# Expert weights in 2 MB tiles, and 21 buffers of 8 KB regrouped as ten of 16 KB and one of 8 KB

## The chip, the cores and the metric

One NeuronCore of a Trainium2 chip runs the kernel: TensorE (PE; its weight loads are listed as PEld), VectorE (DVE), ScalarE (ACT), GpSimd (POOL), SyncE (SP, which issues most transfers here), and 16 DMA engines that move data between HBM and the core's memory of 128 partitions. The metric is the device time of one execution in microseconds, lower being better. The kernel before was timed three times: 1330.16, 1330.19 and 1331.1 us, median 1330.19 us.

## What is computed

One decoder layer for 256 tokens of width 1024, all weights in float32: a combined projection, a Mamba-2 mixer and a sliding-window attention side by side, a gated merge, an output projection, and a mixture of 32 experts of which each token takes 4. Cut to what matters here:

```python
p = x @ W_in                      # 1024 -> [z | xBC | dt | q | k | v | gate_ssm | gate_attn]
s = mamba2(z, xBC, dt)            # causal conv, chunked scan, gate, RMS norm
a = sliding_window_attention(q, k, v)
m = (sigmoid(gate_ssm) * (s @ P_ssm) + sigmoid(gate_attn) * (a @ P_attn)) @ W_o
h = layer_norm(alpha * x + m)
# experts: top 4 of 32
hgu = h[tokens of e] @ w_gate_up[e] + b_gate_up[e]      # 1024 x 2048 per expert: 8 MB
act = glu * sigmoid(1.702 * glu) * (lin + 1)
y_e = act @ w_down[e] + b_down[e]                       # 1024 x 1024 per expert: 4 MB
y   = layer_norm(alpha * h + sum_k gate_k * y_e(k))
```

The expert weights are 32 x 12 MB, 402.65 million bytes; everything else that is loaded is about 60 million bytes.

## The kernel before, in words

**Buffers.** Nearly everything large lies in one pool of 21 buffers of 8 KB per partition (1 MB each, `gtile`): raw weight tiles as they land, their split parts, activations, and later the expert weights. A buffer is handed on when the last instruction on it has run, and the transfer or the write that takes it next waits for that.

**The first stages.** The list `stream` holds 50 weight tiles of 1 MB for the projections: 34 of `w_in` (k, v, then c and q mixed, eight of z, eight of g), 4 of `w_attn_out`, 8 of `w_ssm_out` (tiles 38 to 45) and 4 of `w_mix` (tiles 46 to 49). For float32 accuracy each raw tile is split in two: ACT writes `whi` (rounded), DVE writes `wlo` = raw - `whi`, and PE multiplies three products (`mm3`). `take()` hands PE the next tile: in `weights`, SP is first told to load up to `ahead` tiles further, and `split_ahead` then emits the splits up to `la` tiles further (2 in most stages, 1 in the z stage, 4 at the end). Small pieces of the mixer and the attention are emitted between the matmuls of the weight tiles (`tick`, `side`), always in the order of the program on each engine.

**The end of the first stages.** In the loop over `n` PE takes the eight `w_ssm_out` tiles; `merge` then puts the two branches together on DVE and ACT. After that SP loads x, the norm's constants, the router's weights and `b_down`, and PE runs `mix(c, q)`, for two halves `c` of the tokens and four weight tiles `q`, all four of which stay in memory until `mix(1, q)` has used them. Then come the norm, the router (`turn`, `logits`, `top`, `place`) and the first `gather`, in which PE picks the tokens of two experts by a one-hot matrix.

**The experts.** Tiles of 1 MB: 8 per expert for gate and up (`u`, 128 rows of 2048 each, so 8 KB in one run per partition), 4 for down (`d`, 256 rows, two neighbouring rows per partition, 8 KB in one run). The order is u of expert 0, u of expert 1, d of expert 0, u of expert 2, d of expert 1, and so on. SP loads 6 and then 14 of them during the mix stage (`MB`, `PRE`), and keeps 17 ahead from then on (`AH`, 6 near the end, `AL`). The last tile is loaded in two halves. After the last d tile PE adds the last expert's share, and DVE normalises and stores (lines 1185 to 1200).

Of the kernel before, what the change touches and what calls it, by code (L numbers as in the profile page):

```python
# [8 lines left out]
F = mybir.dt.float32  # L9
# [6 lines left out]
P = 128  # L16
D = 1024
# [10 lines left out]
NGRAN = 21  # L28
AH = 17
MA, MB = 4, 6  # L30
# [3 lines left out]
OVER, AL = 27, 6  # L34
DT, DD = 2, 4
D3 = 4
PRE = 14
L1 = 2
AZ, LZ, AG, LG = 2, 1, 3, 2
# [6 lines left out]
def hybrid_layer(ctx, tc, x, w_in, conv_w, conv_b, dt_bias, a_log, d_skip, norm_w, w_ssm_out,  # L46
# [5 lines left out]
    gran = ctx.enter_context(tc.tile_pool(name="gran", bufs=NGRAN))  # L52
# [40 lines left out]
    st = {"dma": 0, "split": 0, "ahead": 3, "la": 1}  # L93
    raws, splits = {}, {}

    def prefetch(upto):
        while st["dma"] < min(upto, len(stream)):
            i = st["dma"]
            ap, nb = stream[i]
            t = gtile(f"raw{i}")  # L100
            t3 = t.rearrange("p (k n) -> p k n", n=nb)
            if len(halves(i)) > 1:
                nk = 2048 // nb // 2
                for k in (slice(0, nk), slice(nk, 2 * nk)):
# [20 lines left out]
    def weights(i):  # L125

        prefetch(i + 1 + st["ahead"])
        if i >= S_E:
            return raws.pop(i).rearrange("p (k n) -> p k n", n=1024)
        split_ahead(i)  # L130
        nb = stream[i][1]
        return tuple(t.rearrange("p (k n) -> p k n", n=nb) for t in splits.pop(i))

    def split_ahead(i):
# [42 lines left out]
    for e in range(NE + 1):  # L177
        for kp in range(8 if e < NE else 0):
            slots.append(("u", e, kp))
            add(w_gate_up[0, e, P * kp:P * (kp + 1)].rearrange("p (h n) -> p h n", h=2), 1024)  # L180
        for kp in range(4 if e else 0):
            slots.append(("d", e - 1, kp))
            add(w_down[0, e - 1, 256 * kp:256 * (kp + 1)].rearrange("(p j) n -> p j n", j=2), 1024)
# [20 lines left out]
    xn = gtile("xn")  # L204
    xn3 = xn.rearrange("p (c d) -> p c d", d=D)
    for c in range(2):
        nc.sync.dma_start(xn3[:, c], x[0, c * P:(c + 1) * P])
    prefetch(2)
# [38 lines left out]
    ii = const.tile([P, 64], F, name="ii")  # L247
    tt(ii, ident[:, 0:64], ident[:, 64:128], OP.add)


    xh = gtile("xh", R).rearrange("p (k t) -> p k t", t=NT)
    xl = gtile("xl", R).rearrange("p (k t) -> p k t", t=NT)
# [144 lines left out]
    BC = gtile("BC").rearrange("p (s g t) -> p s g t", s=2, g=4)  # L397
    xs = [gtile(f"xs{c}") for c in range(2)]
    xd = [gtile(f"xd{c}") for c in range(2)]
# [43 lines left out]
    cb_t = gtile("cbm").rearrange("p (s g t) -> p s g t", s=4, g=4)  # L443
# [27 lines left out]

    def build_a(c, g):
        ah = gtile(f"ah{c}{g}", R)
# [5 lines left out]
        return ah4  # L479

    def ssd(c, g):
        gcs = slice(512 * g, 512 * g + 512)
        yield need(0, ah=1, xe=1 - c)
        ah4 = build_a(c, g)
# [12 lines left out]
        later(1, lambda: done(bank=2, ah=1))  # L497
# [32 lines left out]
    qT = gtile("qT").rearrange("p (b t) -> p b t", t=NT)  # L530
    kv_t = gtile("kv")
# [4 lines left out]
    def attention(kv, b):  # L536
# [83 lines left out]
    sz = []  # L620
# [3 lines left out]
    def gated():  # L624
# [6 lines left out]
        nwb = gtile("nwb")  # L631
        nc.sync.dma_start(nwb, rows(norm_w, DI))
        yield need(1)
        nc.scalar.preload_act_table_set(EXP_LN)
# [3 lines left out]
        for g in range(4):  # L638
            gcs = slice(512 * g, 512 * g + 512)
            if g % 2 == 0:  # L640
                yT[g // 2] = [gtile(f"yt{g}{p_}", R).rearrange("p (b t) -> p b t", t=NT) for p_ in "hl"]
# [17 lines left out]
    st["la"], st["ahead"], st["rate"] = L1, 3, R1  # L659
# [7 lines left out]
    for kind, j in ORDER:  # L667
# [17 lines left out]
        elif kind == "g":  # L685
            if j == 0:
                st["ahead"], st["la"] = AG, LG
            if j % 4 == 0:
                gts.append(gtile(f"gate{j}").rearrange("p (b t) -> p b t", t=NT))
# [17 lines left out]
        else:  # L707
            if j == 0:
                st["rate"], st["ahead"], st["la"] = R2, AZ, LZ
                sz.extend(gtile(f"sz{c}") for c in range(2))  # L710
                start(0, gated())
# [20 lines left out]
    bgn = gran.tile([32, 2048], F, name="bgn", tag="g")  # L732
    nc.sync.dma_start(bgn, b_gate_up[0])
    mrg = gtile("mrg").rearrange("p (b t) -> p b t", t=NT)
# [18 lines left out]
    mh = gtile("mh", R).rearrange("p (b t) -> p b t", t=NT)  # L753
    ml = gtile("ml", R).rearrange("p (b t) -> p b t", t=NT)
# [7 lines left out]

    for n in range(4):
# [467 lines left out]
```

## Time and profile before

| | us |
|---|---|
| median of three runs | 1330.19 |
| the profiled execution | 1330.74 |
| its span in the profile | 1329.0 |
| PE busy in the span | 1251.8 |
| DVE busy | 431.6 |
| ACT busy | 281.2 |
| first matmul with expert weights | 388.35 |
| DMA: moved in the span | 463.34 MB |

The profile is one execution; its span starts with the first instruction and is 1.2 us shorter than the median of the runs. PE's busy time overlaps itself, since matmuls are pipelined, so a PE that is shown busy is not a PE that could do no more. The DMA rows give what the 16 engines moved in each fortieth of a stretch. A row of the timeline is: start, length, engine, line, operation, what it writes and reads, how many such instructions were put together, and in brackets how long the engine sat idle before it and what ended that.

### The profile page before, as it was taken

To read this page: it belongs to the slowest core of one execution; us is meant where nothing else is said; L and a number is where in the kernel's file an instruction comes from. 1 tells how busy PE (TensorE), PEld (TensorE's weight loads), DVE (VectorE), ACT (ScalarE), POOL (GpSimd) and SP (SyncE) were. 2 spreads that over 40 slices of the span, in tenths; PEclk is the share of its full clock that TensorE was granted. 3 is DMA by queue.
4 is the path that set the end of the run, shared out by engine and by line. 5 is a ranking of instruction groups with operands and counts; after the bars stand their busy time and mean duration, and the time that the engine had idled before them with its cause. 6 is when DMAs were issued, how large, how long until landed. Compare 5 with 4: busy or idle time off the path is not lost. (4 is left out here: it accounts for less than half of the span.)

```text
span 1329.0 us, 16490 instructions
## 1 busy us (share of the span) xinstructions
PE 1251.8 (94%) x6864; PEld 668.7 (50%) x6864; DVE 431.6 (32%) x817; ACT 281.2 (21%) x477; POOL 63.1 (5%) x35
## 2 busy tenths in 40 slices
PE   7999999999999999999999989899898989879985
PEld 7998878999864344343343323333242323223321
DVE  6998987665631211111112111111111111111114
ACT  5555555543211110011010101001010101000001
POOL 0044332000000000000000000000000000000000
PEclk9999999999989999999999999999999999989998
DMA  9523334655999999999999999999999999999994
GB/s 302 181 64 105 118 122 147 208 183 186 354 420 418 422 421 420 421 421 420 421 421 421 421 421 420 421 421 421 421 421 421 421 421 421 420 417 421 420 421 197
DMA packets 106232, 463.34 MB, mean 349 GB/s; under 512 B 9948, under 2 KB 48996, under 8 KB 56964
## 3 DMA queue, kind: packets, MB, share of 16 engines
q1 hardware_dynamic: 106148, 462.19, 86.8%
q8 instruction: 57, 0.93, 0.3%
q14 instruction: 27, 0.22, 0.0%
HBM read 461.11 MB, written 1.05 MB: 348 GB/s over the span
## 5 line engine op out<-in xcount | busy, mean ns | idle before, releaser
L76 PE MATMUL u<-raw,xg 128*64 128x512 f32 x2048 | 470.4, 600 | 29.9 <-DMA raw<-in_w_gate_up_dram 29.8
L76 PEld LDWEIGHTS u<-raw,xg 128*64 128x64 f32 x2048 | 137.7, 137 | 331.3 <-issue 233.8
L76 PE MATMUL d<-raw,ac 128*64 128x512 f32 x1024 | 245.9, 606 | 18.7 <-DMA raw<-in_w_down_dram 10.4
L992 DVE COPY gu<-u 128x512 f32<-128x512 f32 x32 | 22.1, 691 | 701.3 <-PE u L76 701.3
L76 PEld LDWEIGHTS d<-raw,ac 128*64 128x64 f32 x1024 | 67.2, 137 | 147.8 <-issue 104.8
L65 DVE TENSOR_TENSOR wlo<-raw,whi 128x2048 fp32r<-128x2048 f32 (+1 forms) x51 | 120.4, 2371 | 13.2 <-ACT whi L62 12.9
L76 PE MATMUL ws<-xh,whi 128*128 128x256 f32 x400 | 101.7, 292 | 1.8 <-ACT whi L62 1.8
L62 ACT ACTIVATE whi<-raw 128x2048 fp32r<-128x2048 f32 (+1 forms) x51 | 95.4, 1875 | 28.5 <-DMA raw<-in_w_in_dram 8.0
L76 PE MATMUL ws<-xl,whi 128*128 128x256 f32 x400 | 98.3, 283 | 0.0
L62 ACT ACTIVATE gu<-u 128x512 f32<-128x512 f32 x32 | 19.1, 597 | 333.5 <-PE u L76 333.5
L76 PEld LDWEIGHTS ws<-xh,whi 128*128 128x128 f32 x400 | 76.9, 192 | 4.3 <-ACT whi L62 2.2
L76 PEld LDWEIGHTS ws<-xl,whi 128*128 128x128 f32 x400 | 76.9, 192 | 0.9 <-issue 0.7
L76 PEld LDWEIGHTS xg<-G,xr 128*128 128x128 f32 x512 | 61.8, 197 | 24.9 <-issue 24.3
L76 PE MATMUL xg<-G,xr 128*128 128x128 f32 x512 | 67.9, 287 | 0.2 <-DVE G L65 0.2
L62 ACT ACTIVATE xg<-xg 128x512 f32<-128x512 f32 x32 | 19.1, 597 | 215.0 <-PE xg L76 215.0
L76 PE MATMUL out<-y,S 64*128 64x512 f32 x256 | 63.6, 615 | 0.8 <-ACT y L62 0.8
L76 PE MATMUL ws<-xh,wlo 128*128 128x256 f32 x400 | 56.2, 283 | 0.0
L62 ACT ACTIVATE hg<-hg 128x512 f32<-128x512 f32 x32 | 20.2, 631 | 149.8 <-DVE hg L69 149.8
L76 PEld LDWEIGHTS ws<-xh,wlo 128*128 128x128 f32 x400 | 51.6, 192 | 0.0
L1004 PEld LDWEIGHTS tu<-ident,gu 128*128 128x128 f32 x256 | 33.2, 208 | 26.3 <-issue 25.2
L1085 POOL IOTA omisc<- 128x192 f32 x1 | 0.3, 295 | 928.4 <-PE u L76 928.4
L76 PEld LDWEIGHTS out<-y,S 64*128 64x128 f32 x256 | 22.0, 186 | 41.9 <-issue 40.2
(248 smaller groups left out, 1172.1 us busy)
## 6 DMA issues: line engine op xcount, KB each, us to landing
raw<-in_w_gate_up_dram SPq DMA_DIRECT2D x256, 1024.0 KB, 19.8
raw<-in_w_down_dram SPq DMA_DIRECT2D x127, 1024.0 KB, 19.8
raw<-in_w_in_dram SPq DMA_DIRECT2D x33, 1024.0 KB, 5.3
raw<-in_w_ssm_out_dram SPq DMA_DIRECT2D x8, 1024.0 KB, 5.1
raw<-in_w_attn_out_dram SPq DMA_DIRECT2D x4, 1024.0 KB, 5.1
raw<-in_w_mix_out_dram SPq DMA_DIRECT2D x4, 1024.0 KB, 5.1
xn<-in_x_dram SPq DMA_DIRECT2D x2, 512.0 KB, 3.8
raw<-in_w_in_dram SPq DMA_DIRECT2D x2, 512.0 KB, 6.1
```

What stands on the lines that cost most here:

```text
L62: return nc.scalar.activation(o, i, func, **kw)
L65: return nc.vector.tensor_tensor(o, a, b, op=op)
L76: return nc.tensor.matmul(o, l, r, start=start, stop=stop)
L992: nc.vector.tensor_copy(t, banks[hf])
L1004: nc.tensor.transpose(pb[:, b], gu[hf][:, o:o + 255:2], ident)
L1085: nc.gpsimd.iota(ios, pattern=[[ns, 2], [1, ns]], base=cap, channel_multiplier=0, allow_small_or_imprecise_dtypes=True)
```

## The change

The pool becomes ten buffers of 16 KB per partition (`ptile`), mostly used as `pair`: two tiles of 8 KB that are taken and given back together (hi and lo of a weight tile, x's two parts, the two gates, and so on), and one lone buffer of 8 KB (`single`: x at first, then k and v, then the residual). Raw weight tiles of the first stages no longer take pool buffers: they alternate between the two halves of one pair, `ring`, and tile i + 2 is loaded when tile i has been split. `la` is 1 from the first tile to the last. An expert tile is 2 MB: two neighbouring gate-and-up rows or four neighbouring down rows per partition, 16 KB in one run, fetched by one transfer; the columns that PE picks from `hn` and `gu` step by 2 and by 4 accordingly. Loads of expert tiles are asked for at places written out by hand (`prefetch(1)` to `prefetch(10)`). The loads of x, the norm's constants and the router's weights (`mix_loads`) move ahead to the third round of the loop over n; `norm_w` is loaded by ACT's queue into the place of `sz[0]`, `b_down` by GpSimd's. The last expert tile is loaded as 1 MB and two halves of 0.5 MB.

```diff
-NGRAN = 21
-AH = 17
-MA, MB = 4, 6
+NPAIR = 10
+AH = 9
-OVER, AL = 27, 6
+OVER, AL = 27, 7
-PRE = 14
-L1 = 2
-AZ, LZ, AG, LG = 2, 1, 3, 2
+L1 = 1
+LZ, LG, LS = 1, 1, 1
...
-    def gtile(name, dt=F):
-        return gran.tile([P, 2048], dt, name=name, tag="g")
+    def ptile(name, dt=F):
+        return gran.tile([P, 4096], dt, name=name, tag="g")
+
+    def pair(name, dt=F):
+        t = ptile(name, dt)
+        return t[:, 0:2048], t[:, 2048:4096]
...
+    single = lone.tile([P, 2048], F, name="single")
+    ring = pair("ring")
+
+    def prefetch_raw():
+
+        while st["dma"] < S_E:
             i = st["dma"]
             ap, nb = stream[i]
+            if i - 2 >= st["split"]:
+                break
+            t = ring[i % 2]
...
+    def prefetch(upto):
+
+        while moe[0] < min(upto, len(stream) - S_E):
+            m = moe[0]
+            ap, nb = stream[S_E + m]
+            t = ptile(f"w{m}").rearrange("p (k n) -> p k n", n=nb)
+            last = S_E + m == len(stream) - 1
+            for ks in (slice(0, 2), slice(2, 3), slice(3, 4)) if last else (slice(0, 4096 // nb),):
+                nc.sync.dma_start(t[:, ks], ap[:, ks])
+            raws[S_E + m] = t
+            moe[0] += 1
...
-        prefetch(i + 1 + st["ahead"])
-        if i >= S_E:
-            return raws.pop(i).rearrange("p (k n) -> p k n", n=1024)
+        prefetch_raw()
         split_ahead(i)
+        prefetch_raw()
...
+    def expert_weights(n):
+
+        m = n // 2
+        prefetch(m + 1 + st["ahead"])
...
-            hi, lo = gtile(f"whi{j}", R), gtile(f"wlo{j}", R)
+            hi, lo = pair(f"w{j}", R)
...
-            add(w_gate_up[0, e, P * kp:P * (kp + 1)].rearrange("p (h n) -> p h n", h=2), 1024)
+            add(w_gate_up[0, e, 256 * kp:256 * (kp + 1)].rearrange("(p j) n -> p j n", j=2), 2048)
...
-            add(w_down[0, e - 1, 256 * kp:256 * (kp + 1)].rearrange("(p j) n -> p j n", j=2), 1024)
+            add(w_down[0, e - 1, 512 * kp:512 * (kp + 1)].rearrange("(p j) n -> p j n", j=4), 1024)
...
+    st["la"] = LS
     for n in range(4):
+        prefetch((0, 1, 2, 2)[n])
...
+        if n == 2:
+            xr, lnc, wr3, br = mix_loads()
...
             if n == 3 and kh == 1:
-                st["la"] = 4
+                prefetch(3)
...
+        if q == 0:
+            prefetch(4)
     mix(1, 0)
     first_norm(0)
+    prefetch(5)
     mix(1, 1)
     resid(1, 0)
-    prefetch(S_E + MB)
+    prefetch(6)
     mix(1, 2)
+    prefetch(7)
     mix(1, 3)
     resid(1, 1)
+    prefetch(10)
...
-                kk = slice((4 * kq + k) * P, (4 * kq + k + 1) * P)
+                o = 256 * (2 * kq + k // 2) + k % 2
                 for c in range(2):
-                    mm(pb[:, k], hn[:, c, kk], G2[:, c], c == 0, c == 1)
+                    mm(pb[:, k], hn[:, c, o:o + 255:2], G2[:, c], c == 0, c == 1)
```

## Rows read from the trace of the kernel before

**Rows 1.** The page's span and the rate of transfers in 40 equal slices.
```profile
span 1329.0 us, 16490 instructions
...
GB/s 302 181 64 105 118 122 147 208 183 186 354 420 418 422 421 420 421 421 420 421 421 421 421 421 420 421 421 421 421 421 421 421 421 421 420 417 421 420 421 197
```

**Rows 2.** Busy time of each engine by stretch; last PE's clock, DMA share, GB/s.
```profile
33.00:166.00 133.00, 128.89 (x1008) 119.97 (x1007) 124.49 (x211) 74.29 (x151) 43.57 (x21) 0.97 0.38 118
166.00:266.00 100.00, 99.94 (x652) 86.91 (x651) 71.77 (x80) 56.74 (x92) 18.63 (x8) 1.00 0.50 159
266.00:347.00 81.00, 81.00 (x677) 80.83 (x676) 48.26 (x56) 33.46 (x33) 0.00 (x0) 1.00 0.61 202
...
410.00:1300.00 890.00, 842.10 (x4006) 313.51 (x4004) 133.56 (x350) 87.28 (x154) 0.29 (x1) 0.99 1.01 421
```

**Rows 3.** Timeline of SP's queue: the issues of two successive experts' gate-and-up tiles.
```profile
562.74 17.72 SPq L107 DMA_DIRECT2D raw<-in_w_gate_up_dram  x8
...
592.56 5.30 SPq L107 DMA_DIRECT2D raw<-in_w_gate_up_dram  x3
```

**Rows 4.** Timeline of PE at the first expert matmuls.
```profile
388.35 3.65 PE L76 MATMUL u<-raw,xg 128*64 128x512 f32 x16
391.93 1.98 PE L76 MATMUL out<-xr,ia 128*128 128x512 f32 x4
```

**Rows 5.** Transfers from 342 to 410 us: the ordinary queue's packets, MB, share.
```profile
q1 hardware_dynamic: 5422, 27.83, 101.1%
```

**Rows 6.** Timeline of PE at the last expert's tiles.
```profile
1303.56 1.94 PE L76 MATMUL d<-raw,ac 128*64 128x512 f32 x8 [0.65 <-DMA raw<-in_w_down_dram]
...
1309.58 3.65 PE L76 MATMUL d<-raw,ac 128*64 128x512 f32 x16
...
1313.99 1.99 PE L76 MATMUL out<-y,S 64*128 64x512 f32 x8 [0.76 <-ACT y L62]
```

**Rows 7.** Packets moved from 560 to 900 us, by size.
```profile
DMA packets 19641, 143.14 MB, mean 421 GB/s; under 512 B 2181, under 2 KB 2181, under 8 KB 2181
```

**Rows 8.** Transfers from 14 to 34 us, tiles of w_in alone: rate in 40 slices, packets.
```profile
GB/s 92 281 371 389 389 373 352 350 348 352 346 348 344 371 338 348 352 356 350 346 348 350 346 348 346 350 346 350 350 346 346 354 346 348 346 346 350 348 352 344
DMA packets 6800, 6.88 MB, mean 344 GB/s; under 512 B 96, under 2 KB 6799, under 8 KB 6799
```

**Rows 9.** The page's transfers by name: count, KB each, median us from issue to landing.
```profile
raw<-in_w_ssm_out_dram SPq DMA_DIRECT2D x8, 1024.0 KB, 5.1
...
xr<-in_x_dram SPq DMA_DIRECT2D x1, 1024.0 KB, 4.9
```

**Rows 10.** Timeline of DVE: the wlo of tile 5, and of tiles 44 and 45.
```profile
37.63 2.28 DVE L65 TENSOR_TENSOR wlo<-raw,whi 128x2048 fp32r<-128x2048 f32 x1
...
326.23 4.49 DVE L65 TENSOR_TENSOR wlo<-raw,whi 128x2048 fp32r<-128x2048 f32 x2
```

**Rows 11.** Timeline of PE: first matmuls that read the wlo of tiles 5 and 45.
```profile
45.71 1.12 PE L76 MATMUL ws<-xh,wlo 128*128 128x256 f32 x8
...
343.53 1.12 PE L76 MATMUL yss<-yt2h,wlo 128*128 128x256 f32 x8
```

**Rows 12.** Timeline of all engines around the mix stage.
```profile
347.37 0.40 PE L76 MATMUL mix<-whi,mh 128*128 128x512 f32 x1
...
349.49 1.92 ACT L62 ACTIVATE whi<-raw 128x2048 fp32r<-128x2048 f32 x1 [1.67 <-DMA raw<-in_w_mix_out_dram]
...
352.08 4.48 DVE L65 TENSOR_TENSOR wlo<-raw,whi 128x2048 fp32r<-128x2048 f32 x2
...
354.42 0.50 PE L76 MATMUL mix<-wlo,mh 128*128 128x512 f32 x1 [1.20 <-DVE wlo L65]
```

**Rows 13.** Timeline of PE: the transposes that follow the last matmul of the mix stage.
```profile
370.65 1.03 PE L851 MATMUL ht<-ident,xr 128*128 128x128 f32 x8
```

**Rows 14.** The page's weight loads of PE with adjoining columns (xg) and with every second (tu).
```profile
L76 PEld LDWEIGHTS xg<-G,xr 128*128 128x128 f32 x512 | 61.8, 197 | 24.9 <-issue 24.3
...
L1004 PEld LDWEIGHTS tu<-ident,gu 128*128 128x128 f32 x256 | 33.2, 208 | 26.3 <-issue 25.2
```

More of the change, by code (lines that the diff above doesn't have):

```diff
@@ L246, in hybrid_layer @@
         nc.vector.memset(io64[:, :, cap:], -5.0)
[L247 to L252, printed above, removed]
+    xh, xl = (t.rearrange("p (k t) -> p k t", t=NT) for t in pair("x", R))
     xb = [bank(f"xt{kk}").rearrange("p (k c t) -> p k c t", k=2, c=2) for kk in range(4)]
@@ L394, in dt_chain @@
         sub_lo(avl, av, avh)
-    BC = gtile("BC").rearrange("p (s g t) -> p s g t", s=2, g=4)
-    xs = [gtile(f"xs{c}") for c in range(2)]
-    xd = [gtile(f"xd{c}") for c in range(2)]
+    sz = pair("sz")
+    BC = sz[1].rearrange("p (s g t) -> p s g t", s=2, g=4)
+    qT, cb_t = pair("qcb")
+    qT = qT.rearrange("p (b t) -> p b t", t=NT)
+    xs = pair("xs")
+    xd = pair("xd")
     def conv_block(blk, ps, dst):
@@ L470, in decays @@
         act(dte, pa[:, 32:64], AF.Exp)
+    ahs = []
     def build_a(c, g):
-        ah = gtile(f"ah{c}{g}", R)
+        if "ah" not in ready:
+            ready.add("ah")
+            ahs.extend(pair("ah", R))
+        ah = ahs.pop(0)
         ah4 = ah.rearrange("p (s h t) -> p s h t", s=2, h=8)
@@ L630, in gated @@
                 later(1, lambda v=v, w=w, k=k: act(w, v, AF.Square, accum_out=ss[:, k:k + 1]))
-        nwb = gtile("nwb")
-        nc.sync.dma_start(nwb, rows(norm_w, DI))
         yield need(1)
+        nwb = sz[0]
+        nc.scalar.dma_start(nwb, rows(norm_w, DI))
         nc.scalar.preload_act_table_set(EXP_LN)
@@ L640, in gated @@
             if g % 2 == 0:
-                yT[g // 2] = [gtile(f"yt{g}{p_}", R).rearrange("p (b t) -> p b t", t=NT) for p_ in "hl"]
+                yT[g // 2] = [t.rearrange("p (b t) -> p b t", t=NT) for t in pair(f"yt{g}", R)]
             for c in range(2):
@@ L656, in gated @@
                 later(1, ev)
-    st["la"], st["ahead"], st["rate"] = L1, 3, R1
+    st["la"], st["rate"] = L1, R1
     gts = []
@@ L686, in hybrid_layer @@
             if j == 0:
-                st["ahead"], st["la"] = AG, LG
-            if j % 4 == 0:
-                gts.append(gtile(f"gate{j}").rearrange("p (b t) -> p b t", t=NT))
+                st["la"] = LG
+                gts.extend(t.rearrange("p (b t) -> p b t", t=NT) for t in pair("gate"))
             def ev(b, ps, j=j):
@@ L708, in hybrid_layer @@
             if j == 0:
-                st["rate"], st["ahead"], st["la"] = R2, AZ, LZ
-                sz.extend(gtile(f"sz{c}") for c in range(2))
+                st["rate"], st["la"] = R2, LZ
                 start(0, gated())
@@ L729, in hybrid_layer @@
             later(2, lambda j=j: ready.add(("z", j)))
-    bgn = gran.tile([32, 2048], F, name="bgn", tag="g")
+    bgn, mrg = pair("mrg")
+    bgn = bgn[0:32]
     nc.sync.dma_start(bgn, b_gate_up[0])
-    mrg = gtile("mrg").rearrange("p (b t) -> p b t", t=NT)
+    mrg = mrg.rearrange("p (b t) -> p b t", t=NT)
     for n in range(4):
@@ L820, in hybrid_layer @@
     posm = const.tile([P, 2, 32], F, name="posm")
-    ones = rt[:, 416:544]
     ia = const.tile([P, P], F, name="ia")
-    lg, mk, rp, ex = (rt[:, 544 + 64 * i:608 + 64 * i].rearrange("p (c e) -> p c e", c=2) for i in range(4))
-    t8, nm, sw = rt[:, 800:816].rearrange("p (c e) -> p c e", c=2), rt[:, 816:818], rt[:, 818:820]
+    ones = const.tile([P, P], F, name="ones")
+    lg, mk = (const.tile([P, 2, 32], F, name=n) for n in ("lg", "mk"))
+    nm, sw = (const.tile([P, 2], F, name=n) for n in ("nm", "sw"))
+    rp, ex = s64("rp").rearrange("p (c e) -> p c e", c=2), gw
+    t8 = s64("t8")[:, 0:16].rearrange("p (c e) -> p c e", c=2)
     ts(ia, ident, ALPHA, None, OP.mult)
@@ L1181, in hybrid_layer @@
             done_d(n, e, cur[0], S)
-    lnd = gtile("lnd").rearrange("p (s d) -> p s d", d=D)
-    nc.sync.dma_start(lnd[:, 0], rows(ln2_g, D))
-    nc.sync.dma_start(lnd[:, 1], rows(ln2_b, D))
-    res = gtile("res").rearrange("p (c d) -> p c d", d=D)
+    lnd, res = (t.rearrange("p (s d) -> p s d", d=D) for t in pair("lnd"))
+    lnd = [lnd[:, 0], lnd[:, 1]]
+    nc.sync.dma_start(lnd[0], rows(ln2_g, D))
+    nc.sync.dma_start(lnd[1], rows(ln2_b, D))
     work = mo
```

153 lines of the change are left out of this document (74 added, 79 removed).

## Prediction

> **What bounds the kernel now.** I read the transfers first. From the tenth slice on they run at about 420 GB/s without a break [rows 1], and from 410 to 1300 us the DMA engines are fully busy while PE, busy time included that only overlaps, is not [rows 2]: the expert stage is bound by the loading of 402.65 MB. One expert's 12.58 MB come every 29.82 us [rows 3], which is 422 GB/s, or 2.485 us for a tile of 1 MB. Before 347 us the picture is the other way round: the transfers run at 118 to 202 GB/s and PE has hardly a gap [rows 2]; that part is bound by PE, with DVE close behind it from 33 to 166 us (124.5 of 133 us, 94%). So the time is the time at which PE gets through the first stages, then the time to load what is not yet in memory, then a tail. A gain must come from loading faster or from having more loaded when the expert stage begins; and what makes PE late in the first stages is paid in full, unless memory holds more by then.
>
> **How much is loaded at the start.** PE begins with the experts at 388.35 us and has used up 2 MB of them at 391.93 [rows 4]. From 342 to 410 us the ordinary queue moved 27.83 MB [rows 5]; 1.05 MB of it is the last mix tile and some 0.4 MB the remainder of the loads before it, so about 26.4 MB of expert weights are in at 410. The other 376.3 MB end with the last half tile. The first d tile of the last expert is waited for until shortly before 1303.56 [rows 6]; three tiles more at 2.485 us make that last landing 1310.9. So 376.3 MB take 900.9 us, starts, stutters and the uneven finish of the engines included.
>
> After the change all ten pairs go to experts: 20.97 MB fit, no more. They are full before PE is done with its first 2 MB tile (see the mix stage below), so that the eleventh tile can only be asked for when 16 matmuls are through, where the old kernel was loading all along. Had it been full at the same moment, about 18.8 MB would have been in (26.4 less 18.1 us at 422 GB/s), so that the preload is worth some 2 MB, or 5 us, not the three tiles that are fetched early. PE releases the next tiles every 4.5 to 5.5 us (16 matmuls are 3.58 us, and the residual adds 1.9 [rows 4]), about what a transfer of 2 MB takes, so little is lost after that.
>
> **Larger packets.** Each transfer ran in packets of 8 KB, and each adds one tiny packet per DMA engine: from 560 to 900 us 17,460 large ones and 2,181 small [rows 7], 8 and 1 per engine and MB. Tiles of 16 KB per partition would halve both: 9 packets fewer per engine and 2 MB. What is a packet's fixed price? Tiles of w_in come in packets of 1 KB, and where these fill the engines the rate settles at 348 GB/s [rows 8]: 3.01 us per MB with 64 packets per engine, against 2.485 us with 8. The difference, 0.53 us over 56 packets, is 9.4 ns each: 85 ns per 2 MB tile, 1.7%, and 15.5 us over the 182 tiles that follow the first ten. From below: a lone MB in 1 KB packets lands in 5.1 us, one in 4 KB packets in 4.9 [rows 9]; that is 4 ns each, or 7 us in all; and nothing at all if long runs are cut at 8 KB. A loss is excluded: fewer packets of the same engines have no price of their own in any row. I take 9.4 ns, since that stretch has full engines as the expert stage has.
>
> [...]
>
> **What the first stages lose.** (a) *Lookahead 1 and two pairs for split weights.* For each of the tiles 2 to 45 I read in the timelines how long before PE's first use its wlo was finished. With lookahead 2 that was 5 to 16 us: 5.8 for tile 5, done at 39.9 and used at 45.7, and 12.8 for tile 45, done at 330.7 and used at 343.5 [rows 10, 11]. One tile less takes a tile's period from this (5.8 to 13 us). What is left is 0 to 7 us for c and q tiles, and 1.4 to 7 us for g to `w_ssm_out`. The z tiles already had lookahead 1 and PE lost nothing there [rows 2]. In the c and q stage DVE has 8.5 us of slack in all [rows 2]; if waiting for whi leaves it idle, PE waits. Bounds 0 and 8.5 us; I take 3.
>
> (b) *The end of the first stages.* In the mix stage PE needs a tile every 2.73 us (12 matmuls), while a tile needs ACT for 1.9 and DVE for 2.24 us, and the load of mix tile 3 now waits until tile 1 in the same half of the ring is split. The chain from 347.4, when PE starts mix tile 0 and frees a pair: whi of tile 1 until 349.3, the last `merge` about 1 us, wlo until 352.5, load of tile 3 5.1 us, whi and wlo until 361.8; then PE has that tile and the second half's four left, 13.6 us: 375.4. The old kernel split these tiles ahead, lost 1.2 us [rows 12] and ended at 370.65 [rows 13]. That is 4.8 us. Before it, SP now puts 4.3 MB (an expert tile, x, the norm's constants, the router: some 10 us of transfers) ahead of the raw tile 45, which can be asked for at about 329, when tile 43 is split, and which PE wants split from 341.6 on: 0 to 4 us more. SP issues in order, so an expert tile without a free pair holds up the raw tile behind it; the third one waits for the pair that PE frees with tile 44 at 341.6, and holds mix tile 3, which waits longer for the ring anyway. I take 6.5 for the whole, bounds 3 and 9. The expert tiles that are asked for on the way (at about 311, 323, 346, 353 and 362, then as pairs are freed up to 375) are all in by about 398.
>
> (c) *Strided columns.* The 32 matmuls of the first gather read every second column; such a weight load takes 208 ns, an even one 197 [rows 14]: 0.4 us. Later ones lie under the transfers.
>
> (d) *No price, with their cover:* `norm_w` is asked for on ACT's queue one step (2.9 us of PE) before DVE reads it, and a lone MB lands in 5.1 us [rows 9]: at worst 2.2 us of DVE, which has 28 of 100 us idle there [rows 2]. `b_down` is asked for on an idle GpSimd before the experts begin.
>
> **The tail.** With 2 MB the last but one tile holds two quarters of the last expert, and lands whole 4.9 us before the last piece. Then come four times 1.94 us of d, 1.99 of out and 0.44 of S: 10.2 us, so PE ends 5.3 us after the last landing, where it was 2.3 (1309.58 + 3.65 [rows 6], against 1310.9). The remaining 15.8 us to the span's end stay. Price 3 us.
>
> **The sum.** First release 391.93 + 0.4 + 3 + 6.5 = 401.8. Issue and first byte 1.8 (most of the 2.1 by which a lone MB's 5.1 us exceed its 3.0): 403.6. The remaining 381.7 MB at the old pace 913.8, less 15.5 for packets: 898.3, so the last landing is at 1301.9. Tail 5.3 + 15.8: the span is 1323.0. The profiled execution took 1330.74 for its 1329.0 of span; the median lies 1.2 above the span: **1324 us**, 6 us or 0.5% less.
>
> **The rivals.**
> - *Packets save next to nothing* (runs cut at 8 KB, or a price that grows with bytes): then the sum gives 1324 + 15.5 = 1339, slower. It decides from a saving below 51 ns per tile, at which 1330 is reached. For it: lone transfers show 4 ns (1332). Against it: the full engines' 348 against 422 GB/s. This is also how the change would fail to do what it says.
> - *DVE becomes the bound of the c and q stage*, because each split now waits for a pair and for PE: 8.5 us instead of 3, and 9 instead of 6.5 in (b): 1332. For it: 94% busy [rows 2]. Against it: the z stage.
> - *The first stages lose next to nothing*, splits being hidden as in the z stage and only the mix chain costing 3 us: 1324 - 6.5 = 1317. For it: PE's waits on splits are short now. Against it: the mix chain above.
>
> **How the numbers follow.** My forecast has 48% (1318 to 1329), the first rival 17% (1331 to 1339), the second 17% (1329 to 1335), the third 18% (1312 to 1318). The range 1313 to 1337 leaves out the outer ends of the first and third rival. A measurement here can tell about 0.2% from no change, so faster is under 1327.5: most of the forecast (41%) and the third rival, 59%. Within 0.2%: the rest of the forecast and parts of the first two rivals, 18%. Slower, above 1332.9: 23%.
>
> **What would show it.** Packets of 16 KB and about 4.92 us between issues of expert tiles, 428 GB/s where it was 421; a dip of the transfers just before the first expert tile is released, at about 402 us; PE idle before wlo in the mix stage and `ht` at 377 to 380 us; some idle DVE before 166 us; the last d matmul some 5 us behind the last landing. I am wrong if the rate stays at 422 GB/s, if `ht` starts before 373 or after 385, or if PE rather than the transfers ends the expert stage.

## The result, and the profile after

| kernel | us, median (lowest to highest) | against before (95% interval) |
|---|---|---|
| before | 1330.59 (1330.16 to 1331.10) | |
| changed | 1339.11 (1337.41 to 1339.88) | 1.0062 (1.0045 to 1.0080) |
| predicted | 1324 (1313 to 1337) | |

The change makes the kernel 8.5 us slower, where 6 us less were forecast; the time lies outside the range. The profiled execution took 1339.34 us for a span of 1337.6. First the page of the changed kernel, to set beside [rows 1]: span, rate of transfers in 40 equal slices, packets.

```profile
span 1337.6 us, 16127 instructions
...
GB/s 227 159 126 97 121 99 126 189 166 238 319 342 335 383 429 431 431 431 430 430 430 430 430 430 431 430 430 431 430 431 431 431 431 430 431 427 430 430 430 172
DMA packets 78741, 463.30 MB, mean 346 GB/s; under 512 B 6908, under 2 KB 45956, under 8 KB 53924
```

From the fifteenth slice on the loads are faster than before, 430 against 421. The loss lies between slices 11 and 14, at 319 to 383, where the old kernel ran at 354 and then 420. The same by stretches, to set beside [rows 2] (stretch, length, busy time of PE, its weight loads, DVE, ACT and POOL, then PE's granted clock, DMA share, GB/s):

```profile
33.00:166.00 133.00, 126.63 (x992) 118.12 (x990) 123.57 (x208) 75.67 (x151) 43.04 (x19) 0.97 0.40 124
166.00:266.00 100.00, 98.29 (x606) 83.94 (x607) 65.51 (x79) 51.59 (x89) 21.29 (x10) 0.97 0.45 144
266.00:347.00 81.00, 81.00 (x676) 80.52 (x675) 49.42 (x55) 33.56 (x35) 0.00 (x0) 1.00 0.66 227
347.00:410.00 63.00, 48.45 (x245) 40.15 (x244) 30.69 (x62) 13.68 (x16) 1.16 (x2) 0.86 0.86 332
410.00:460.00 50.00, 50.00 (x235) 21.08 (x236) 9.28 (x30) 7.30 (x13) 0.00 (x0) 0.97 0.89 335
460.00:1300.00 840.00, 800.26 (x3836) 305.56 (x3834) 121.23 (x318) 81.41 (x145) 0.30 (x1) 1.00 1.01 430
```

The kernel before, from 347 on:

```profile
347.00:410.00 63.00, 59.21 (x273) 38.40 (x273) 23.30 (x63) 10.00 (x18) 0.00 (x0) 0.93 1.01 419
410.00:460.00 50.00, 50.00 (x248) 20.09 (x246) 11.63 (x30) 5.55 (x10) 0.00 (x0) 0.99 1.01 419
```

PE idles 14.6 of the 63 us from 347 on, where it had idled 3.8, and the DMA engines stand too (0.86, then 0.89, where they had been at 1.01). Its timeline there (start, length; in brackets the idle time before and what ended it), to set beside [rows 4, 12, 13]:

```profile
353.68 2.57 PE L79 MATMUL yss<-yt,w 128*128 128x256 f32 x16 [3.65 <-ACT w L65]
...
366.74 5.58 PE L79 MATMUL mix<-w,m 128*128 128x512 f32 x23 [2.16 <-DVE w L68]
376.72 0.79 PE L79 MATMUL mix<-w,m 128*128 128x512 f32 x1 [4.40 <-ACT w L65]
379.05 15.31 PE L79 MATMUL mix<-w,m 128*128 128x512 f32 x59 [1.53 <-DVE w L68]
...
394.20 1.03 PE L883 MATMUL ht<-ident,single 128*128 128x128 f32 x8
...
411.90 3.65 PE L79 MATMUL u<-w,xg 128*64 128x512 f32 x16
415.49 1.98 PE L79 MATMUL out<-single,ia 128*128 128x512 f32 x4
```

Each wait up to 379 us is for a split weight tile. `ht` starts 23.5 us later than in [rows 13], the first expert matmul 23.5 us later than in [rows 4]. The expert period on SP's queue, to set beside [rows 3]: 29.12 us, where it was 29.82.

```profile
773.28 14.87 SPq L126 DMA_DIRECT2D w<-in_w_gate_up_dram  x4
...
802.40 0.33 SPq L126 DMA_DIRECT2D w<-in_w_gate_up_dram  x1
```

And the tail, to set beside [rows 6]:

```profile
1312.02 1.94 PE L79 MATMUL d<-w,ac 128*64 128x512 f32 x8 [0.81 <-DMA w<-in_w_down_dram]
...
1318.04 3.65 PE L79 MATMUL d<-w,ac 128*64 128x512 f32 x16
1322.45 1.99 PE L79 MATMUL out<-y,S 64*128 64x512 f32 x8 [0.76 <-ACT y L65]
```

**Where the 8.5 us come from.** From 415 to 460 us the ordinary queue moved 15.52 MB on top of the ten tiles (20.97 MB), so 36.5 MB are in at 460. Before, it moved 20.91 MB from 410 to 460, on top of some 26.4: 47.3 MB. The 10.8 MB that are missing are 25 us of loading. The other 366 MB (29.1 experts) come 0.70 us per expert sooner: 20.4 us. The tail is 3 us longer. 25 - 20.4 + 3 is some 8 us, of 8.5 measured. So the change gave what was hoped for from loading, and gave back more ahead of it. Two questions follow: what makes the first stages late, and what makes the loads faster.

### The profile page after: what moved, and what is told of

The parts are those of the page before. It is cut to its first block, busy times and chain, and to the rows that moved or that the text cites. A ratio compares the mean times of both kernels' runs of the same rounds, so it can differ in the third digit from the quotient of the medians.

```text
span 1337.6 us, 16127 instructions
## 1 busy us (share of the span) xinstructions
PE 1252.5 (94%) x6864; PEld 682.1 (51%) x6864; DVE 431.6 (32%) x816; ACT 282.9 (21%) x477; POOL 66.4 (5%) x37
## 5 line engine op out<-in xcount | busy, mean ns | idle before, releaser
L79 PE MATMUL u<-w,xg 128*64 128x512 f32 x2048 | 464.5, 598 | 22.1 <-DMA w<-in_w_gate_up_dram 22.1
L79 PEld LDWEIGHTS u<-w,xg 128*64 128x64 f32 x2048 | 140.2, 137 | 314.7 <-issue 263.5
L79 PE MATMUL d<-w,ac 128*64 128x512 f32 x1024 | 241.1, 602 | 19.7 <-DVE gg L73 10.3
L79 PE MATMUL ws<-x,w 128*128 128x256 f32 x1200 | 154.9, 289 | 2.8 <-ACT w L65 2.5
L79 PEld LDWEIGHTS ws<-x,w 128*128 128x128 f32 x1200 | 149.3, 195 | 6.1 <-ACT w L65 2.8
L79 PEld LDWEIGHTS d<-w,ac 128*64 128x64 f32 x1024 | 68.5, 137 | 142.3 <-issue 125.1
L68 DVE TENSOR_TENSOR w<-ring,w 128x2048 fp32r<-128x2048 f32 (+1 forms) x51 | 119.6, 2349 | 25.9 <-ACT w L65 25.7
L65 ACT ACTIVATE w<-ring 128x2048 fp32r<-128x2048 f32 (+1 forms) x51 | 95.8, 1878 | 76.0 <-DMA ring<-in_w_ssm_out_dram 13.1
L79 PE MATMUL xg<-G,single 128*128 128x128 f32 x512 | 70.5, 292 | 0.2 <-DVE G L68 0.2
L79 PE MATMUL out<-y,S 64*128 64x512 f32 (+1 forms) x264 | 67.6, 616 | 0.8 <-ACT y L65 0.8
```

Source lines behind the costliest of these rows:

```text
L65: return nc.scalar.activation(o, i, func, **kw)
L68: return nc.vector.tensor_tensor(o, a, b, op=op)
L79: return nc.tensor.matmul(o, l, r, start=start, stop=stop)
```

## Experiments

Starts of PE's first matmuls of `w_ssm_out` (yss), of the mix stage (mix) and of the experts (u), and the transposes after the mix stage (ht), in each kernel's trace, with its median time:

| kernel | yss | mix | ht | u | us |
|---|---|---|---|---|---|
| before | 299.1 | 347.4 | 370.7 | 388.4 | 1330.6 |
| changed | 307.3 | 361.4 | 394.2 | 411.9 | 1339.1 |
| e2: before, lookahead 1 | 294.8 | 343.0 | 367.3 | 385.0 | 1328.0 |
| e7: e2, two pairs for split tiles | 309.5 | 357.8 | 382.0 | 399.6 | 1351.0, with 17 other buffers |
| e8: e2, two raw tiles | 295.8 | 344.1 | 368.4 | 386.2 | 1327.7 |
| e3: changed, raw tiles first | 304.9 | 353.2 | 384.9 | 402.6 | 1331.8 |
| e4: changed, mix tiles in pairs | 305.0 | 353.3 | 376.4 | 394.7 | 1322.6 |
| e9: e4, `b_down` on SP, used later | 307.7 | 356.0 | 379.2 | 396.0 | 1321.9 |
| e14: before, 64 bytes further | 298.0 | 346.3 | 368.7 | 386.9 | 1316.2 |

Kernels with the same code up to yss differ by up to 3.5 us there (e4, e5, e9: 304.2 to 307.7); smaller differences say nothing.

### What makes the first stages late

**e2, lookahead 1 on the old buffers.**

```diff
-L1 = 2
+L1 = 1
-AZ, LZ, AG, LG = 2, 1, 3, 2
+AZ, LZ, AG, LG = 2, 1, 3, 1
...
-                st["la"] = 4
+                st["la"] = 1
```

> The kernel before with lookahead 1 in every stage (2 in the c, q and g stages before, 4 for the mix tiles); its 21 buffers of 8 KB and its raw tiles loaded 2 to 4 ahead stay. If the lookahead alone makes the first stages late: PE idles at the entry of the z stage (8 us) and in the mix stage, and the first u matmul comes at 400 us or later instead of 388.35. If it is the ring of two raw tiles or the early expert loads: at 388 to 392 us. The whole time would move less than the start of the experts, since 21 MB are not full before about 397 us here: 1330 to 1333 us.

1327.98 us (1326.58 to 1331.49), u at 385.0: nothing is late, rather 3 us earlier. The lookahead costs nothing by itself. That leaves what the change shares out: two pairs for split tiles, and two raw tiles.

**e7, two pairs for split tiles, and e8, two raw tiles, each on e2 (one run each).**

```diff
+            if j < S_MIX:
+                t = wpool.tile([P, 4096], R, name=f"w{j}", tag="wp")   # e7: 2 of these, 17 other buffers
+                hi, lo = t[:, 0:2048], t[:, 2048:4096]
...
-        prefetch(i + 1 + st["ahead"])
+        prefetch(min(st["split"] + 2, S_E))                            # e8: ahead of and behind split_ahead
```

> The kernel before with lookahead 1 (first mix matmul at 343.0, none late), with whi and wlo in two pairs of their own up to w_ssm_out, each free only when PE is through with both halves; 17 buffers for all else, so that the experts' part says nothing. Raw tiles are still loaded 2 to 4 ahead. If the two pairs make the stages up to w_ssm_out late in the changed kernel: idle PE from 100 to 175 us and the first mix matmul at 348 to 353. If not: 343 to 345.

> The kernel before with lookahead 1, and raw tiles asked for at most two beyond the last split one, as the changed kernel's ring does, in the first stages; whi and wlo lie in any of the 21 buffers. The mix stage's early expert loads fall away, so that the experts' part says little. If the ring makes the stages up to w_ssm_out late: first mix matmul at 348 to 353. If not: 343 to 345, and only the mix stage is longer than 24.3 us, as mix tiles 2 and 3 wait for the ring.

Two stretches of each, e7 first, then e8 (columns as above):

```profile
100.00:166.00 66.00, 60.37 (x438) 53.32 (x436) 59.86 (x95) 37.97 (x84) 29.15 (x13) 0.97 0.29 96
166.00:200.00 34.00, 32.96 (x160) 25.67 (x161) 25.88 (x43) 15.18 (x34) 7.32 (x5) 0.91 0.35 125
```

```profile
100.00:166.00 66.00, 64.74 (x474) 57.06 (x473) 63.02 (x102) 38.56 (x85) 28.64 (x14) 1.00 0.34 112
166.00:200.00 34.00, 34.00 (x187) 27.36 (x187) 31.55 (x42) 20.27 (x41) 9.14 (x4) 1.00 0.36 124
```

With two raw tiles PE works on as in e2 (mix at 344.1). With two pairs it idles 5.6 of the 66 us and its granted clock falls to 0.91 in the z stage (mix at 357.8). The split of a tile can't start until PE has left the tile before last. PE doesn't wait long for the split itself here, but for the mixer's and the attention's pieces that stand behind it in the order of ACT and DVE. One such place in e7:

```profile
161.93 1.91 ACT L63 ACTIVATE w<-raw 128x2048 fp32r<-128x2048 f32 x1 [2.54 <-PE z L77]
163.75 0.58 ACT L63 ACTIVATE sc<-pt 128x512 f32<-128x512 f32 x1
...
164.38 0.66 PE L584 MATMUL pt<-ident,sc 128*128 128x128 f32 x4 [1.61 <-ACT sc L63]
```

From 100 to 200 us PE waits 2.4 and 1.6 us for ACT's `sc` and 1.6 for DVE's `xd` in e7, and the changed kernel has the same three waits; of these e8 has only one, of 0.4 for `sc`. This is the changed kernel's picture: 8.2 us late at yss. The size is not the same: e7 is 14.7 us later there than e2, and 10.4 later than the kernel before.

**e3, raw tiles first, and e4, mix tiles in pairs of their own.** e3 takes the three early expert tiles and `mix_loads` behind the last raw tiles. e4 does so too, gives the two free pairs to the four raw mix tiles, and splits two ahead.

```diff
-        prefetch((0, 1, 2, 2)[n])
...
-        if n == 2:
-            xr, lnc, wr3, br = mix_loads()
...
-            if n == 3 and kh == 1:
-                prefetch(3)
...
+    xr, lnc, wr3, br = mix_loads()        # behind the loop over n
...
+        if n in (1, 2):                   # e4 alone
+            mraw.extend(pair(f"mr{n}"))   # raw mix tiles go there, not into the ring
...
+            if n == 3 and kh == 0:
+                st["la"] = 2
```

> The changed kernel with expert tiles 0 to 2 and the loads of x, the norm's constants and the router asked for behind the last raw tiles instead of ahead of them. If this traffic makes the raw tiles late (4.3 MB and SP's wait for the third pair): the first u matmul comes 5 to 8 us earlier, at 404 to 407 us, and the time falls by as much, to 1331 to 1334 us. If the ring of two and lookahead 1 do it: 410 to 412 us and 1337 to 1340 us. The entry of the z stage is late by either, as nothing changes there.

> The changed kernel with the four raw mix tiles loaded early into two pairs of their own (where expert tiles 0 and 1 lay), split two ahead, and all expert tiles asked for behind them, from about 345 us on. If the end of the first stages is late because mix tiles come through the ring one by one: the mix stage takes about 24 us instead of 32.8, and 6 us at the last w_ssm_out tile return as well: the first u matmul at 396 to 399 us. If a late start of the experts is paid one for one: 1324 to 1327 us. If what is lost is the time in which the loads stand (ten pairs full or not yet free), less comes back, since the expert loads now start 25 us later: 1330 to 1336 us.

e3: u at 402.6, 9.3 us earlier; 1331.77 us (1328.07 to 1343.34; the spread is taken up below), 7.3 less. e4: u at 394.7, 17.2 us earlier; 1322.62 us, 16.5 less, and ratio 0.9937 (0.9924 to 0.9950) to the kernel before. So the late first expert is paid about one for one, and e4 beats both kernels. PE in e4's mix stage, which takes 23.2 us instead of 32.8:

```profile
353.27 5.86 PE L79 MATMUL mix<-w,m 128*128 128x512 f32 x25
360.22 16.39 PE L79 MATMUL mix<-w,m 128*128 128x512 f32 x71 [1.09 <-DVE w L68]
376.45 1.03 PE L886 MATMUL ht<-ident,single 128*128 128x128 f32 x8
```

In e3, where mix tiles still came through the ring, the stage took 31.7. The 23.5 us are then: some 8 from the two pairs up to yss, some 7 from traffic ahead of the last raw tiles (mix 14.0 us late, 8.2 of which it had at yss, and 1.1 in the mix stage), 8.5 from mix tiles through the ring (31.7 - 23.2).

**e6 and e11, splits in halves** (e6: z and mix tiles, on e5 below; e11: mix tiles alone, on e9).

```diff
-        return [slice(0, 1024), slice(1024, 2048)] if i == 0 else [slice(0, 2048)]
+        return [slice(0, 1024), slice(1024, 2048)] if i == 0 or i >= S_MIX else [slice(0, 2048)]   # e11
```

> The same, with b_down on SP's queue, and the z and mix tiles split in two halves each, so that DVE begins with the first half while ACT is at the second and PE begins with the first wlo half. If the time from a free pair to the split tile (1.9 us of ACT, then 2.3 of DVE) makes the z and mix stages late: the first u matmul comes 3 to 6 us earlier than 394.7, and the time is 1317 to 1320 us. If it is the amount of DVE work around 160 to 175 us: nothing earlier, 1322 to 1325 us, as 12 more instructions each on ACT and DVE cost a little.

> The kernel with mix pairs and b_down used late, and the four mix tiles split in halves, the z tiles whole. With both in halves the mix stage took 21.8 us instead of 23.2, but the z stage grew by 4 us. If the halves shorten the mix stage alone: the first u matmul 1.4 us earlier than without them and the time 1 to 2 us less, 1319 to 1322. If the expert stage is not bound by that start: no difference.

In both the mix stage takes 21.8 us instead of 23.2. e6 (1337.40, stopped by `b_down` as e5) has yss at 308.6, 4.4 us later than e5: the z stage gains nothing. e11: 1322.98 (1321.44 to 1324.41) against e9's 1321.94: a gain of 1.4 us in the stage doesn't show in the time.

### What makes the loads faster

**e1, runs of 8 KB, and e10, transfers of 1 MB as well.** Same tiles and buffers as the changed kernel.

```diff
-...rearrange("(p j) n -> p j n", j=2), 2048)     # u: one run of 16 KB per partition
+...rearrange("(j p) n -> p j n", j=2), 2048)     # two of 8 KB; d likewise
 
-                nc.sync.dma_start(t, ap)
+                for a in range(2):                # e10
+                    nc.sync.dma_start(t[:, a], ap[:, a])
```

> The changed kernel with the same 2 MB tiles, buffers and order, but each partition takes its 16 KB as two runs of 8 KB from two places in memory (other rows of the weights lie on the partitions). If the packets bring the gain: 29.1 us per expert go back to about 29.8, 182 tiles x 0.108 us = 19.7 us, so 1339.1 + 19.7 = 1359 us; with the 85 ns per tile of the prediction 1354.6. If it is the size of the transfer (one issue for 2 MB) that brings it: 29.1 us per expert and 1339 us as before. The first u matmul stays at 412 us by either.

> The changed kernel with runs of 8 KB as in the kernel with two runs per partition (1342.9 us, 427 GB/s), and each 2 MB tile as two transfers of 1 MB; buffers and order are the changed kernel's. If the number of transfers costs (one more small packet and switch per engine and MB): 421 GB/s as in the kernel before, 0.07 us more per tile, 1342.9 + 12.7 = 1355.6 us. If it does not, and the kernel before is slower because of its small buffers: 427 GB/s and 1343 us.

e1: 1342.86 us (1340.59 to 1344.04), 3.75 more, with u 1.8 us earlier. e10: 1342.01 (1340.97 to 1343.75). Both at 427 GB/s. So packets of 16 KB give some 5.6 us, which is 4 ns for each of the eight packets saved per tile; transfers of 2 MB give nothing (1342.9 us against 1342.0). Two thirds of the gain in rate are in neither. e10 loads as the kernel before does, packet for packet, and yet at 427 instead of 421.

**e13, a pause in the kernel before.** The author's guess was that its engines ran out of step with each other, and that a dry queue would set them right.

```diff
-        prefetch(i + 1 + st["ahead"])
+        if H0 < n < H1:                   # 17 tiles are not asked for
+            hold.extend(gtile("hold") for _ in range(3 if n == H0 + 2 else 1))
+        else:
+            prefetch(i + 1 + st["ahead"])
...
+                at(n + 1, lambda: [nc.vector.tensor_copy(h[:, 0:1], y[:, 0:1]) for h in hold])
```

> The kernel before, unchanged up to the eleventh expert; there 17 tiles' requests are held back (their buffers are taken by empty tiles) until PE has used the last tile that was asked for, at about 740 us, so that the DMA engines stand for a moment and all begin anew; then all goes on as before, with the same buffers, transfers of 1 MB and packets of 8 KB. The stand costs 3 to 6 us. If the kernel before is slow because its engines run out of step (8 KB packets of 312 to 319 ns beside 309): 420 to 421 GB/s ahead of the pause, 426 to 427 behind it, 570 us x 1.4% = 8 us gained, 1325 to 1329 us in all. If its buffers or its layout make it slow: 420 to 421 GB/s on both sides and 1334 to 1337 us.

1335.88 us (1334.75 to 1336.31). The stretches around the pause:

```profile
600.00:700.00 100.00, 100.00 (x493) 39.05 (x490) 16.04 (x43) 10.12 (x18) 0.00 (x0) 1.00 1.01 421
...
720.00:740.00 20.00, 14.16 (x58) 4.67 (x56) 5.73 (x31) 2.22 (x4) 0.00 (x0) 0.91 0.73 293
...
800.00:900.00 100.00, 93.89 (x448) 34.61 (x446) 12.36 (x32) 9.04 (x16) 0.00 (x0) 1.00 1.01 421
```

The queue ran dry (0.73), and it is 421 GB/s on both sides. That theory falls. What is left are the buffers. Laid out, those of the kernel before begin at byte 22464 of each partition, those of the changed kernel at 23296, because small tiles ahead of them differ; nothing in the diff shown speaks of it.

**e14, e18, e16, e15, e17: the buffers moved.** e14 and e18 are the kernel before with 64 and 192 unused bytes ahead of its buffers, e16 is e10 with 64, e17 is e2 with 64; e15 is e9 with one small tile moved behind the pairs.

```diff
+    const.tile([P, 16], F, name="shift")      # e18: [P, 48]
     ident = const.tile([P, P], F, name="ident")
```

> The kernel before with 64 unused bytes per partition ahead of its buffers. As the programs are laid out, its 21 buffers begin at byte 22464 of each partition and every 8192 on, a multiple of 64 but not of 128; the changed kernel's pairs begin at 23296, a multiple of 256. With the 64 bytes they begin at 22528, a multiple of 256 too. If the place of the buffers makes the packets of 8 KB take 312 to 319 ns instead of 309: all at 309 ns and 427 GB/s; 376 MB at 427 instead of 421 GB/s are 12.5 us less: 1318 us. If the offsets between the engines, the number of buffers or their use do it: 421 GB/s and 1330 to 1331 us.

> The reverse: the changed kernel with transfers of 1 MB and packets of 8 KB (427 GB/s, 1342 us), with the 64 unused bytes, which put its pairs at byte 23360, a multiple of 64 but not of 128. If the place of the buffers sets the rate: 421 GB/s again and 1342 + 12.5 = 1354.5 us. If not: 427 GB/s and 1342 us.

> The kernel before with 192 unused bytes ahead of its buffers, which puts them at byte 22656, a multiple of 128 but not of 256. With 64 bytes (a multiple of 256) it ran at 427 GB/s and 1316 us, with none (an odd multiple of 64) at 421 and 1330.6. If a multiple of 128 is enough: 309 ns and 1316 to 1317 us. If it takes 256: packets above 309 ns and a time between 1318 and 1331 us.

> The kernel before with lookahead 1 (1328 us) and the 64 unused bytes: the same 12.5 us less by the place of the buffers, 1315 to 1317 us, which would beat every kernel so far with tiles of 1 MB. If the place is not the cause: 1328 us.

> The kernel with mix pairs and b_down used late (1322 us, packets of 16 KB in 611 ns), with one small tile moved so that the pairs begin at byte 23040, a multiple of 512, instead of 23296, a multiple of 256 only. If a multiple of 256 is enough: 611 ns, 430 GB/s and 1321 to 1323 us. If a multiple of 512 saves more: packets below 609 ns, 432 GB/s or more and 1316 to 1319 us.

| kernel | buffers begin at | GB/s | us (lowest to highest) |
|---|---|---|---|
| before | 22464 = 256 x 87 + 192 | 421 | 1330.6 |
| e18 | 22656 = 256 x 88 + 128 | 421 | 1329.94 (1329.41 to 1332.35) |
| e14 | 22528 = 256 x 88 | 427 | 1316.24 (1316.03 to 1317.35) |
| e17 | 22528 | 427 | 1316.42 (1313.33 to 1317.66) |
| e10 | 23296 = 256 x 91 | 427 | 1342.01 |
| e16 | 23360 = 256 x 91 + 64 | 421 | 1355.90 (1353.15 to 1356.75) |
| e9 (16 KB) | 23296 | 430 | 1321.94 |
| e15 (16 KB) | 23040 = 512 x 45 | 430 | 1322.10 (1321.52 to 1324.18) |

Packets of 8 KB from 500 to 600 us and the ordinary queue's packets, MB and share, first e14's, then e16's:

```profile
DMA packets 5855, 42.67 MB, mean 427 GB/s; under 512 B 650, under 2 KB 650, under 8 KB 650
...
q1 hardware_dynamic: 5851, 42.61, 100.9%
```

```profile
DMA packets 5774, 42.08 MB, mean 421 GB/s; under 512 B 640, under 2 KB 640, under 8 KB 640
...
q1 hardware_dynamic: 5769, 42.02, 101.0%
```

64 bytes make the kernel before 14.3 us faster (ratio 0.9894, 0.9879 to 0.9909) and e10 13.9 us slower. The places at a multiple of 256 gave 427 GB/s (22528, 23296), the three behind one 421 (22464, 22656, 23360); a multiple of 128 alone has no part of the gain (e18), and e15's 23040, a multiple of 512, no more than e9's 23296 (both 430). 16 engines x 100 us x 1.009, less 650 small packets of 9 ns (the mean of the kernel before's), over e14's 5201 large ones is 309 ns a packet; e16's 1.010 over 5129 is 314, and so is the mean in the records of the kernel before. The 64 bytes move the small tiles behind them too, but it is the packets into these buffers that change their time. Packets of 16 KB were not tried off a multiple of 256. e14 is the best kernel here, with the old tiles of 1 MB; e17 is no better. With both at a multiple of 256, the change costs 1339.1 - 1316.2 = 23 us.

The loss did not grow with the distance behind a multiple of 256: 64 (e16), 128 (e18) and 192 bytes (before) all gave 421 GB/s.

### A second queue beside the full one

e4's one traced run took 1340.55 us, its five others 1321 to 1323; e3's runs spread in the same way. The trace of that run, from 420 to 520 us and from 700 to 800:

```profile
DMA packets 2587, 37.68 MB, mean 377 GB/s; under 512 B 287, under 2 KB 287, under 8 KB 287
...
q1 hardware_dynamic: 2583, 37.62, 100.4%
```

```profile
DMA packets 2959, 43.07 MB, mean 431 GB/s; under 512 B 330, under 2 KB 330, under 8 KB 330
...
q1 hardware_dynamic: 2955, 43.01, 100.6%
```

The engines are busy throughout in both. 16 engines x 100 us x 1.004 over 2296 large packets is 700 ns each, and 613 in the later stretch. The slow packets begin at 392 us, while `b_down` moves on GpSimd's queue (391.8 to 394.7), and end at about 546; the 402 and 556 us in e5's expectation are 10 us too late. e3's traced run (1343.34 us) is alike: `b_down` at 400.7 to 403.5, packets of 681 ns from then to 555.

**e5, `b_down` on SP's queue; e9, the same with a tile of its own, used at step 20 instead of 6; e12, e9 with seven such loads on GpSimd's queue for no use.**

```diff
-            nc.gpsimd.dma_start(bd[hf][0:32], b_down[0, :, 512 * hf:512 * hf + 512])
+            nc.sync.dma_start(bd[hf][0:32], b_down[0, :, 512 * hf:512 * hf + 512])   # e5
...
-    at(6, bias_down, pre=False)
+    at(20, bias_down, pre=False)                                                     # e9
...
+    for n_ in range(30, 350, 50):                                                    # e12
+        at(n_, lambda: nc.gpsimd.dma_start(XG["bdt"], b_down[0]))
```

> The kernel with mix tiles in pairs of their own, but b_down is loaded on SP's queue behind expert tile 9, not on GpSimd's. In that kernel's profile the 16 KB packets take 611 ns up to 402 us, where the 4 KB packets of b_down run on GpSimd's queue, and 694 to 704 ns from then to 556 us (376 instead of 430 GB/s), which is about 18 us of transfers: it took 1340.55 us, its other runs 1321 to 1323. If b_down on a second queue puts the engines out of step: packets stay at 611 ns and every run lies at 1321 to 1324. If the cause is another (PE's reads, the full queue): the slow packets are there again in some run, at 1335 us or more.

> The kernel with mix tiles in pairs of their own; b_down goes on SP's queue behind expert tile 9 into a tile of its own, and its product is made at step 20 instead of 6, so that PE no longer waits for it (that wait stood from 411 to 420 us in the run with the load on SP's queue). If a second queue's transfers put the engines out of step: 16 KB packets stay at 611 ns after 400 us, and all runs lie at 1320 to 1324 us. If the slow packets have another cause: some run of five or more at 1330 or above.

> The same kernel with b_down loaded again, for no use, seven times during the expert stage, by GpSimd's queue (0.13 MB each, at every 50th step). The bytes are worth 0.3 us each, 2 us in all: 1323 to 1326 us if a second queue costs only its bytes. If it puts the engines out of step: 16 KB packets of about 680 to 704 ns behind some of these loads, for tens of us, and runs that lie at 1330 to 1370 us and differ by 5 us and more among themselves.

e5: 1335.61 us (1331.78 to 1339.42), slower by another cause: `b_down` lies behind ten tiles in one queue, PE waits for it 8.3 us in the traced run, and meanwhile frees no tile.

```profile
PE out L79 <- DMA y<-in_b_down_dram: 8.3, 1, 8.3
```

e9: 1321.94 (1320.89 to 1323.82), no stretch of slow packets behind 400 us. e12: 1330.25 (1328.17 to 1332.07), 8.3 us more where its bytes are worth 2. Its loads did not come at every 50th step: GpSimd, which has little else to do, issued six of the seven between 447 and 486 us, each as soon as the one before had landed, and the seventh at 1175. The stretch of the six, e12's and then e9's:

```profile
450.00:500.00 50.00, 50.00 (x248) 19.78 (x248) 8.37 (x22) 5.02 (x9) 2.46 (x5) 1.00 1.01 393
```

```profile
450.00:500.00 50.00, 50.00 (x248) 19.68 (x246) 8.36 (x22) 5.61 (x10) 0.00 (x0) 1.00 1.01 430
```

The ordinary queue moved 18.83 MB there, e9's 21.48: 6.2 of the 8.3 us, 1.8 of them for the bytes. Packets of 700 ns and more run beside each of the six; behind the second they stay until the third, behind the others they are gone within some 2 us. So beside a second queue's transfers the full queue's packets got slower (700 ns and more in e12, 611 in e9), and that queue stayed in the slower pattern or fell back. The kernels with `b_down` on SP's queue have no such stretch in their traces (e5, e6, e9, e11, e15). What ends it, and why it lasted some 155 us in the traced runs of e3 and e4 and not in e12, stays open.

## Why the prediction was wrong

- **Rate.** 15.5 us were taken for packets, and about 20 came; the size was nearly right by luck, the cause was not. Packets of 16 KB save 4 ns each (5.6 us in all, e1), the lower figure of the prediction, which it took from lone loads [rows 9]; 9.4 ns from the 1 KB packets [rows 8] do not hold for large ones. The other two thirds are the place of the buffers (14.3 us in e14), for which the prediction had no term.
- **(a) Lookahead 1 and two pairs, 3 us taken: 8.2 us.** The failed step is the slack: it was read as the time from the finished wlo to PE's use [rows 10, 11], less one tile. That counts when a split is asked for, not when it can start. With two pairs ACT's part of a split waits for PE itself, and the pieces behind it on ACT and DVE come late to PE. "The z tiles already had lookahead 1 and PE lost nothing there" [rows 2] did not carry over, because those tiles had free buffers (e2, e7). As the same code gives 304.2 to 307.7 us at yss, 8.2 stands for 5 to 9.
- **(b) The end, 6.5 us taken, at most 9: 15.3 us.** The mechanism was right; its two terms were too small. Mix tiles through the ring cost 8.5, not 4.8: the chain reckoned with a load of 5.1 us, where the page of the changed kernel has 7.2 for mix tiles, and with matmuls at the old pace, where PE's granted clock was 0.79 and 0.87 from 370 to 390 us, behind the waits of 4.40 and 1.53. Traffic cost some 7, not 0 to 4.
- **Restart.** "Little is lost" after the first release was wrong by 6.7 us: from about 417, when the loads began anew, to 460 us 15.5 MB came, where 430 GB/s would be 18.4. PE had ten tiles to work off and was never idle there, but freed a pair only every 5.4 us (nine issues from 415.60 to 458.57), where a load takes 4.9: between its tiles lay the first experts' gathers, the residual and 4.00 us for `b_down`. In e9, whose first release came at 399.68 us, before the queue was empty, and whose `b_down` comes later, the rate is 421 from 417 to 460 us.
- **Tail, 3 us taken:** PE gets the last but one tile at 1312.02 and ends its last d matmul at 1321.7. If the last 2 MB took another 4.9 us, as in the full stream (an estimate), they landed at 1316.9, and PE ends 4.8 us behind them, where 5.3 was predicted and 2.3 had been before: as predicted. From PE's last `out` to the span's end nothing changed (8.5 and 8.6 us later than before).
- **The sum.** Predicted 45.1 MB in at 460 us (restart at 403.6); it was 36.5. 8.6 MB are 20 us, against 5 us more gained by the rate: 1324 + 15 = 1339. The first rival has 1339 as well, but by luck: its rate of 422 GB/s did not come. The second had (a) about right, at 8.5, and (b) too small, at 9. Of the signs named ahead, 428 GB/s and the dip came (430, and at 413 instead of 402); `ht` after 385 was named as refuting it, and came at 394.2.

## What to carry over

Before crediting larger packets or tiles with a faster stream, look where the buffers begin: moved to a multiple of 256 bytes, the old kernel gained more than any regrouping here (14.3 us in e14, 8.7 in e9). Slack read from a trace holds only for the buffers it was measured with (3 us were reckoned from it, 8.2 came): when they are fewer, ask from which event on the work can start at all. In the changed kernel the last of the ten pairs was asked for at 395 us, 17 us ahead of the first expert matmul; that delay was paid about one for one (e4 began the experts 17.2 us earlier and took 16.5 less), and the restart behind it cost another 6.7 us.

## What the runs showed of the hardware

- Packets of 8 KB into buffers that begin 64 (e16), 128 (e18) or 192 bytes (the kernel before) behind a multiple of 256 ran at 421 GB/s, at each of the three, and into buffers that begin at such a multiple (e14, e17, e10) at 427, 1.4% faster.
- Two transfers of 1 MB loaded as fast as one of 2 MB with the queue full (e10 and e1: 1342.0 and 1342.9 us, both 427 GB/s).
- A full queue's 16 KB packets went from 611 to some 680 (e3) or 700 ns (e4) and stayed there for some 155 us, at full DMA share, after transfers on another queue.
- Behind two short waits PE was slower in the changed kernel's z stage: 12 matmuls of the same form took 3.00 us ahead of the two, of 1.61 us each, and 5.06 behind them:

```profile
160.62 3.00 PE L79 MATMUL z<-w,x 128*128 128x512 f32 x12
...
166.11 0.66 PE L609 MATMUL pt<-ident,sc 128*128 128x128 f32 x4 [1.61 <-ACT sc L65]
...
168.78 1.19 PE L79 MATMUL s<-single,qcb 64*128 64x128 f32 x6 [1.61 <-DVE xd L68]
169.90 5.06 PE L79 MATMUL z<-w,x 128*128 128x512 f32 x12
```

The granted clock of these stretches (the figure ahead of the DMA share) is 0.75 and then 0.57, where the kernel before had 1.00 in both; the changed kernel first:

```profile
165.00:170.00 5.00, 2.29 (x13) 1.74 (x13) 5.00 (x8) 2.63 (x5) 5.00 (x3) 0.75 0.51 191
170.00:175.00 5.00, 5.00 (x14) 3.67 (x16) 4.86 (x9) 0.00 (x0) 0.91 (x1) 0.57 0.15 22
```

```profile
165.00:170.00 5.00, 5.00 (x22) 3.21 (x22) 4.77 (x8) 2.67 (x3) 3.24 (x2) 1.00 0.18 68
170.00:175.00 5.00, 5.00 (x28) 3.66 (x27) 3.46 (x8) 2.50 (x11) 0.00 (x0) 1.00 0.00 0
```
